# Exchanged matmul operands for the picked experts' weights, with a ScalarE copy of one one-hot table

## The chip, the core and the metric

The kernel runs on one core of a Trainium2 chip. The metric is the device time of one launch in microseconds (us), taken as the median of several runs. The engines are TensorE (PE in the profile, PEld for its weight loads), VectorE (DVE), ScalarE (ACT), GpSimd (POOL) and SyncE (SP, which issues the DMAs).

## The reference, cut to what matters

The program is a stack of three blocks on 256 tokens of width 1024. The change touches the expert layer of the first block only, `peer`. Each token takes, for each of 8 heads, 16 of 16,384 experts, where an expert is a pair of keys out of 128 and 128:

```python
def peer(h, w_pq, sub_keys, expert_u, expert_v):
    def one(xb):                                            # 128 tokens
        q = (xb @ w_pq).reshape(PEER_BLOCK, PEER_HEADS, 2, PEER_DKH)
        s = jnp.einsum('thpd,hpkd->thpk', q, sub_keys)
        sv, si = lax.top_k(s, PEER_TOPK)                    # 16 keys of each side
        cand = sv[:, :, 0, :, None] + sv[:, :, 1, None, :]
        cidx = si[:, :, 0, :, None] * N_KEYS + si[:, :, 1, None, :]
        best, pos = lax.top_k(cand..., PEER_TOPK)           # 16 experts of a head
        eidx = jnp.take_along_axis(cidx, pos, axis=-1)
        g = jax.nn.softmax(best, axis=-1)
        act = jax.nn.gelu(jnp.einsum('thkd,td->thk', expert_u[eidx], xb))
        return jnp.einsum('thk,thkd->td', g * act, expert_v[eidx])
```

## The kernel before, in words

The kernel does not gather experts. It multiplies all 128 x 128 experts with the tokens: `up(j)` makes the products of the 128 experts that have second key `j` (24 matmuls of 256 columns, since each product is made of three, high by high, high by low, low by high), ScalarE takes the gelu, and the result stands in `H[first key, j, token]`. Column `j` is then multiplied by a weight that is zero for all but the picked experts, and a last pass multiplies by `expert_v`.

The weights come from one-hot tables. A column of picks (8 heads by 16 picks) lies on the 128 partitions. For four tokens, `prepare` lets VectorE write two tables of float16 into `oo[pick, which key, key, token]`: a one where the pick's first key (`oo[:, 0]`) or second key (`oo[:, 1]`) equals the column (line 957). It multiplies `oo[:, 1]` with the pick's weight, which stands as a high and a low float16 part, into `ow` (line 959, two instructions). `group` then makes, for each of the four tokens, a 128 x 128 table of weights in PSUM by two matmuls, high and low part: `oo[:, 0]` of the token is the stationary operand, `ow` the moving one. In both tables the token is the innermost index, so the 128 keys of one token stand 4 elements, 8 bytes, apart, and a matmul's moving operand spreads over 1,024 bytes of each partition. The helper `shared` (lines 281 to 291) asks for one load of the stationary operand for both matmuls.

There are 64 groups (256 tokens by four). They lie between the 92 calls of `up` for `j` = 36 to 127; with `GR = 82` most calls have a `prepare` ahead and a `group` behind them (64 of 82), and the others have none. `PD = 1` puts a group one call behind its `prepare`. `drain` multiplies a finished PSUM table into `H`: VectorE for the columns that have their gelu already (lines 942 and 945), ScalarE copies the rest (line 948). A call of `up` needs its weights split: ScalarE rounds a loaded tile (line 302, tile `wh`), VectorE subtracts (line 306, tile `wl`). There are two buffers of each, so a split waits until TensorE is done with the call before last. Line 989 and 992 are the gelu, line 990 multiplies it with weights that are there already.

The code is recorded in program order, and a scheduler of the framework sets the final order of each engine's queue; each engine then works strictly in that order. `oo`, `ow` and the gelu's tile `k` share one pool of 6 buffers.

Of the kernel before, what the change touches and what calls it, by code (L numbers as in the profile page):

```python
# [12 lines left out]
F16 = mybir.dt.float16  # L13
U32 = mybir.dt.uint32
AF = mybir.ActivationFunctionType
OP = mybir.AluOpType
# [3 lines left out]
P = 128  # L20
# [239 lines left out]
class Kern:  # L260
# [16 lines left out]

    def mm(self, out, l, r, start=True, stop=True):
        self.nc.tensor.matmul(out, l, r, start=start, stop=stop, skip_group_check=True)  # L279

    def shared(self, l, jobs):

        t = self.nc.tensor
        for n, (out, r, start, stop) in enumerate(jobs):
            if n == 0:
                first = t.matmul(out, l, r, start=start, stop=stop, skip_group_check=True).ins  # L286
            else:
                t.add_instruction(mybir.InstMatmult(  # L288
                    name=self.nc.get_next_instruction_name(), engine=first.engine, start_tensor_calc=start,
                    stop_tensor_calc=stop, tile_size=first.tile_size, tile_position=first.tile_position,  # L290
                    bass_skip_group_check=True, ldweights=False, ins=[t.lower_ap(r), first.ins[1]],
                    outs=[t.lower_ap(out)]))

    def split(self, src, shape, hi="act", lo="dve"):
        d = self.SS(shape)
# [544 lines left out]
    def peer(self, ys, gb):  # L840


        nc, tc, I = self.nc, self.tc, self.I
        st = ExitStack()
        pool = st.enter_context(tc.tile_pool(name="pe", bufs=1, reuse_waits="tile"))
# [15 lines left out]
        W2 = pool.tile([P, 2, T], F16, name="W2")  # L861
# [76 lines left out]
        def drain():  # L938
            nonlocal toks
            pg, ts = pend.pop(0)  # L940
            pv = pg.rearrange("p (t j) -> p j t", t=4)
            nc.vector.scalar_tensor_tensor(H1[:, :, ts], pv[:, :NJ1], 1.0 / WS, H1[:, :, ts], op0=OP.mult, op1=OP.mult)
            m = cols - NJ1
            if m:
                nc.vector.scalar_tensor_tensor(H2[:, :m, ts], pv[:, NJ1:cols], 1.0 / WS, H2[:, :m, ts],
                                               op0=OP.mult, op1=OP.mult)
            if cols < NKEY:
                nc.scalar.activation(H2[:, m:, ts], pv[:, cols:], AF.Copy, scale=1.0 / WS)
            toks = ts.stop

        def prepare(t0):
            ts = slice(t0, t0 + 4)
            B = [P, P, 4]
            oo = pool.tile([P, 2, P, 4], F16, tag="k2", name="oo", bufs=6)
            ow = pool.tile([P, 2, P, 4], F16, tag="k2", name="ow", bufs=6)
            for i in (1, 0):
                nc.vector.tensor_tensor(oo[:, i], iota, IJ[:, i, None, ts].to_broadcast(B), op=OP.is_equal)
            for h in range(2):
                nc.vector.tensor_tensor(ow[:, h], oo[:, 1], W2[:, h, None, ts].to_broadcast(B), op=OP.mult)
            ready.append((oo, ow, ts))  # L960

        def group():
            oo, ow, ts = ready.pop(0)
            pg = self.bank()
            for i in range(4):
                self.shared(oo[:, 0, :, i], [(pg[:, i * P:(i + 1) * P], ow[:, h, :, i], h == 0, h == 1)
                                             for h in range(2)])
            pend.append((pg, ts))
            if len(pend) > LAG:
                drain()  # L970
# [10 lines left out]
        n, ready = 0, []  # L981
        for j in range(NJ1, NKEY):
            while n < 64 and n * GR < (j + 1 - NJ1 - GD) * 64:
                prepare(4 * n)
                n += 1
            pa = up(j, "dve" if j % PLO else "pool")
            if toks:
                ga = K1([P, T], F32)
                nc.scalar.activation(ga[:, :toks], pa[:, :toks], AF.Gelu)
                nc.vector.tensor_tensor(Hj(j)[:, :toks], ga[:, :toks], Hj(j)[:, :toks], op=OP.mult)  # L990
            if toks < T:
                nc.scalar.activation(Hj(j)[:, toks:], pa[:, toks:], AF.Gelu)
            cols = j + 1
            while len(ready) > (PD if n < 64 else 0):
                group()
            if n == 64 and not ready and pend:
                drain()
            if toks == T and j >= NKEY - VP:
                part(order[len(parted)])
# [1046 lines left out]
```

## Time and profile before

| | |
|---|---|
| median of 3 runs | 1917.75 us (1917.72 to 1919.15) |
| profiled execution | 1914.85 us, span 1913.1 us |
| TensorE busy | 1847.9 us (97%) |
| VectorE busy | 1304.5 us (68%) |
| ScalarE busy | 970.0 us (51%) |
| GpSimd busy | 176.9 us (9%) |

The profile is of one execution, and its own time is 1914.85 us. A record of a matmul lasts longer than the matmul holds the array: successive records overlap, so the distance from start to start is what a matmul costs in a full queue. In rows of matmuls the moving operand stands first behind the arrow and the stationary one second. Weight loads have records of their own (PEld), which also overlap.

### The profile page before, as it was taken

The numbers are of one execution on the slowest core, as the hardware profiler recorded it, in microseconds if no ns is written. First come the engines' busy times: TensorE is split into PE (matmuls) and PEld (weight loads), VectorE is DVE, ScalarE is ACT, GpSimd is POOL, SyncE is SP. The second block draws the span as 40 slices with busy tenths as digits, with TensorE's granted clock in tenths as the row PEclk, the third lists the DMA queues.
The fourth block names the chain that finished last, engine by engine and source line by source line (L and its number), as shares of the span: only waits on it lengthen the run. The fifth ranks groups of instructions, "written<-read, shape, count | busy, mean of one in ns | idle before, by whom it ended". The sixth has DMA issues, their size and how long they took to land.

```text
span 1913.1 us, 32724 instructions
## 1 busy us (share of the span) xinstructions
PE 1847.9 (97%) x12634; PEld 1645.1 (86%) x12634; DVE 1304.5 (68%) x3029; ACT 970.0 (51%) x1792; POOL 176.9 (9%) x119
## 2 busy tenths in 40 slices
PE   7999989999999999999999999998999999989998
PEld 6775579999999999888888789987999899879997
DVE  4536668987777887555555666677787656767785
ACT  4535444443444444544444546455666564456663
POOL 0000003320000000000000003320100033200000
PEclk9999999999999999999999999999999999999999
DMA  8732544543444445655555654313666234125671
GB/s 306 252 110 89 172 149 141 180 167 125 150 145 151 147 146 166 207 189 190 188 188 180 218 180 129 122 56 100 201 226 224 89 111 133 67 78 176 196 231 59
DMA packets 85100, 302.92 MB, mean 158 GB/s; under 512 B 10096, under 2 KB 10992, under 8 KB 84816
## 3 DMA queue, kind: packets, MB, share of 16 engines
q1 hardware_dynamic: 84944, 300.83, 48.0%
q8 instruction: 99, 1.62, 0.3%
q14 instruction: 57, 0.47, 0.1%
HBM read 298.56 MB, written 2.10 MB: 157 GB/s over the span
## 4 chain that ended last, share of the span: by engine, by line
PE 83%; DVE 11%; ACT 3%; DMA 1%; issue 1%; SPq 0%; POOLq 0%; POOL 0%; DVEq 0%; ACTq 0%
PE b L274 21%; PE b L276 21%; PE b L275 21%; PE b L279 13%; DVE wl L306 3%; PE b L286 2%; PE b L288 2%; PE b L1171 1%; PE b L537 1%; ACT wh L302 1%; PE b L1362 1%; DVE eq L1102 0%; DMA raw<-in_wv 0%; DVE tm L1035 0%; DVE u L1991 0%
## 5 line engine op out<-in xcount | busy, mean ns | idle before, releaser
L302 ACT ACTIVATE wh<-raw 128x1024 fp32r<-128x1024 f32 x457 | 483.8, 1060 | 562.1 <-PE b L275 265.9
L306 DVE TENSOR_TENSOR wl<-raw,wh 128x1024 fp32r<-128x1024 f32 x414 | 523.8, 1266 | 269.0 <-ACT wh L302 268.5
L276 PE MATMUL b<-r,wl 128*128 128x256 f32 (+1 forms) x1216 | 345.1, 284 | 9.8 <-DVE wl L306 9.8
L274 PE MATMUL b<-r,wh 128*128 128x256 f32 (+1 forms) x1216 | 351.0, 289 | 0.0
L275 PE MATMUL b<-r,wh 128*128 128x256 f32 x1152 | 323.1, 280 | 0.0
L274 PE MATMUL b<-hh,wh 128*128 128x256 f32 x1056 | 301.6, 286 | 1.8 <-DVE ast L1687 1.8
L276 PE MATMUL b<-hh,wl 128*128 128x256 f32 x1056 | 299.6, 284 | 1.8 <-DVE wl L306 1.7
L275 PE MATMUL b<-hl,wh 128*128 128x256 f32 x1056 | 298.6, 283 | 0.0
L276 PEld LDWEIGHTS b<-r,wl 128*128 128x128 f32 x1216 | 230.3, 189 | 12.6 <-DVE wl L306 11.0
L274 PEld LDWEIGHTS b<-r,wh 128*128 128x128 f32 x1216 | 231.4, 190 | 3.2 <-issue 1.5
L306 POOL TENSOR_TENSOR wl<-raw,wh 128x1024 fp32r<-128x1024 f32 x43 | 106.2, 2470 | 1240.0 <-ACT wh L302 960.1
L275 PEld LDWEIGHTS b<-r,wh 128*128 128x128 f32 x1152 | 218.4, 190 | 0.0
L274 PEld LDWEIGHTS b<-hh,wh 128*128 128x128 f32 x1056 | 202.2, 191 | 4.6 <-DVE ast L1687 2.3
L276 PEld LDWEIGHTS b<-hh,wl 128*128 128x128 f32 x1056 | 202.2, 191 | 3.1 <-DVE wl L306 3.0
L275 PEld LDWEIGHTS b<-hl,wh 128*128 128x128 f32 x1056 | 202.3, 192 | 1.4
L275 PE MATMUL b<-wl,k 128*128 128x512 f32 x492 | 194.8, 396 | 0.8 <-DVE wl L306 0.8
L274 PE MATMUL b<-wh,k 128*128 128x512 f32 x492 | 194.8, 396 | 0.0
L276 PE MATMUL b<-wh,k 128*128 128x512 f32 x492 | 194.6, 395 | 0.0
L275 PEld LDWEIGHTS b<-wl,k 128*128 128x128 f32 x492 | 92.4, 188 | 23.7 <-DVE wl L306 1.5
L274 PEld LDWEIGHTS b<-wh,k 128*128 128x128 f32 x492 | 92.4, 188 | 22.6 <-ACT wh L302 0.3
L276 PEld LDWEIGHTS b<-wh,k 128*128 128x128 f32 x492 | 92.4, 188 | 22.3
L1991 DVE SCALAR_TENSOR_TENSOR u<-b,vec,u 128x255 f32<-128x255 f32 (+1 forms) x176 | 84.3, 479 | 9.1 <-ACT u L1989 6.5
(493 smaller groups left out, 3091.8 us busy)
## 6 DMA issues: line engine op xcount, KB each, us to landing
raw<-in_eu SPq DMA_DIRECT2D x128, 512.0 KB, 3.9
raw<-in_ev SPq DMA_DIRECT2D x128, 512.0 KB, 3.5
raw<-in_fi SPq DMA_DIRECT2D x88, 512.0 KB, 4.4
raw<-in_w_ada SPq DMA_DIRECT2D x48, 512.0 KB, 5.6
raw<-in_wi SPq DMA_DIRECT2D x48, 512.0 KB, 3.8
raw<-in_fo SPq DMA_DIRECT2D x44, 512.0 KB, 4.6
raw<-in_w SPq DMA_DIRECT2D x16, 512.0 KB, 6.2
raw<-in_w_pq SPq DMA_DIRECT2D x16, 512.0 KB, 4.2
```

The lines of the kernel that those rows point to most:

```text
L274: mm(out, L.hi, R.hi, start=start, stop=False, skip_group_check=True)
L275: mm(out, L.hi, R.lo, start=False, stop=False, skip_group_check=True)
L276: self.lastmm = mm(out, L.lo, R.hi, start=False, stop=stop, skip_group_check=True)
L279: self.nc.tensor.matmul(out, l, r, start=start, stop=stop, skip_group_check=True)
L286: first = t.matmul(out, l, r, start=start, stop=stop, skip_group_check=True).ins
L288: t.add_instruction(mybir.InstMatmult(name=self.nc.get_next_instruction_name(), engine=first.engine, start_tensor_calc=start, stop_tensor_ ...
L302: nc.scalar.activation(dst.hi, src, AF.Copy)
L306: e.tensor_tensor(dst.lo, src, dst.hi.bitcast(F32), op=OP.subtract)
L537: nc.tensor.matmul(pa[32 * j:32 * j + 32, :P], self.s2[:, 4 * h + k], wa[:, k, m * P:(m + 1) * P], start=(k == 0), stop=(k == 3), tile_pos ...
L1171: nc.tensor.matmul(pa[32 * j:32 * j + 32], self.s2[:, k], wa[:, j % 2 * 512:(j % 2 + 1) * 512], start=(k == 0), stop=(k == KD - 1), tile_p ...
L1362: nc.tensor.transpose(pt[:, sc * P:(sc + 1) * P], Pm[:, sc * P:(sc + 1) * P], self.ident)
L1991: nc.vector.scalar_tensor_tensor(u[:, g, j:], src[:, :T - j], self.v2("fc", (2 - j) * 44 + i), u[:, g, j:], op0=OP.mult, op1=OP.add)
```

## The change

The operands change places. The weights are now multiplied into the first key's table (`oo[:, 0]`), and `ow` becomes the stationary operand, in its old layout with 4 elements between the keys of a token. The plain table of the second key moves; ScalarE first copies it into a new tile `oc[pick, token, key]`, in which the 128 keys of a token lie side by side (256 bytes). `oc` has a pool of 3 buffers of its own. `shared` goes, and the ordinary helper `mm` makes the eight matmuls of a group, each with its own stationary operand. The sums are the same.

```diff
-    def shared(self, l, jobs):
...
             for h in range(2):
-                nc.vector.tensor_tensor(ow[:, h], oo[:, 1], W2[:, h, None, ts].to_broadcast(B), op=OP.mult)
-            ready.append((oo, ow, ts))
+                nc.vector.tensor_tensor(ow[:, h], oo[:, 0], W2[:, h, None, ts].to_broadcast(B), op=OP.mult)
+            oc = pool.tile([P, 4, P], F16, tag="oc", name="oc", bufs=3)
+            nc.scalar.activation(oc, oo[:, 1].rearrange("p i t -> p t i"), AF.Copy)
+            ready.append((oc, ow, ts))
...
             for i in range(4):
-                self.shared(oo[:, 0, :, i], [(pg[:, i * P:(i + 1) * P], ow[:, h, :, i], h == 0, h == 1)
-                                             for h in range(2)])
+                for h in range(2):
+                    self.mm(pg[:, i * P:(i + 1) * P], ow[:, h, :, i], oo[:, i], start=h == 0, stop=h == 1)
```

In the new program lines stand 13 lower up to `prepare` and 10 or 11 lower behind it: 302 and 306 become 289 and 293, 942, 945 and 948 become 929, 932 and 935, 957 and 959 become 944 and 946, 989, 990 and 992 become 978, 979 and 981. The copy to `oc` is line 948 of the new program.

TensorE's queue at the first group, before (the end of a call of `up`, then weight loads and matmuls in pairs):

```order
L276 MATMUL b_4894<-r_2441,wl_4891 128x256
L286 LDWEIGHTS oo_4844
L286 MATMUL b_4920<-ow_4845,oo_4844 128x128
L288 LDWEIGHTS oo_4844
L288 MATMUL b_4920<-ow_4845,oo_4844 128x128
L286 LDWEIGHTS oo_4844
L286 MATMUL b_4920<-ow_4845,oo_4844 128x128
```

The same place of the new program:

```order
L276 MATMUL b_4898<-r_2441,wl_4895 128x256
L279 LDWEIGHTS ow_4845
L279 MATMUL b_4924<-oc_4850,ow_4845 128x128
L279 LDWEIGHTS ow_4845
L279 MATMUL b_4924<-oc_4850,ow_4845 128x128
L279 LDWEIGHTS ow_4845
L279 MATMUL b_4924<-oc_4850,ow_4845 128x128
```

The number of loads and of matmuls is the same, and both programs load weights ahead of each matmul, the one with `shared` too.

VectorE's queue over one group in the middle of the stretch, before (`H1` and `H2` are the two parts of `H`):

```order
L942 SCALAR_TENSOR_TENSOR H1_2627<-b_6416,H1_2627 128x36x4
L957 TENSOR_TENSOR oo_6428<-iota_2622,IJ_2618 128x512
L990 TENSOR_TENSOR H2_4843<-k1_6412,H2_4843 128x84
L945 SCALAR_TENSOR_TENSOR H2_4843<-b_6222,H2_4843 128x33x4
L957 TENSOR_TENSOR oo_6428<-iota_2622,IJ_2618 128x512
L959 TENSOR_TENSOR ow_6429<-oo_6428,W2_2619 128x512 x2
L306 TENSOR_TENSOR wl_6490<-raw_6487,wh_6489 128x1024
```

The same place of the new program:

```order
L929 SCALAR_TENSOR_TENSOR H1_2627<-b_6468,H1_2627 128x36x4
L944 TENSOR_TENSOR oo_6480<-iota_2622,IJ_2618 128x512
L979 TENSOR_TENSOR H2_4843<-k1_6464,H2_4843 128x84
L932 SCALAR_TENSOR_TENSOR H2_4843<-b_6268,H2_4843 128x33x4
L944 TENSOR_TENSOR oo_6480<-iota_2622,IJ_2618 128x512
L293 TENSOR_TENSOR wl_6546<-raw_6543,wh_6545 128x1024
L946 TENSOR_TENSOR ow_6481<-oo_6480,W2_2619 128x512 x2
```

The split of the weights (`wl`) now stands ahead of the two multiplications into `ow`.

ScalarE's queue at the same place, before:

```order
L302 ACTIVATE wh_6436<-raw_6434 128x1024
L989 ACTIVATE k1_6371<-b_6346 128x84
L992 ACTIVATE H2_4843<-b_6346 128x172
L302 ACTIVATE wh_6489<-raw_6487 128x1024
L989 ACTIVATE k1_6412<-b_6387 128x84
L992 ACTIVATE H2_4843<-b_6387 128x172
L948 ACTIVATE H2_4843<-b_6222 128x59x4
L302 ACTIVATE wh_6542<-raw_6540 128x1024
```

The same place of the new program:

```order
L289 ACTIVATE wh_6490<-raw_6488 128x1024
L978 ACTIVATE k1_6421<-b_6396 128x84
L981 ACTIVATE H2_4843<-b_6396 128x172
L948 ACTIVATE oc_6431<-oo_6425 128x512
L289 ACTIVATE wh_6545<-raw_6543 128x1024
L978 ACTIVATE k1_6464<-b_6439 128x84
L981 ACTIVATE H2_4843<-b_6439 128x172
L948 ACTIVATE oc_6486<-oo_6480 128x512
L935 ACTIVATE H2_4843<-b_6268 128x59x4
L289 ACTIVATE wh_6600<-raw_6598 128x1024
```

Each copy to `oc` stands behind the gelu of a call and ahead of the next copy out of PSUM and the next split.

## Rows read from the trace of the kernel before

**Rows 1.** The page: busy us, share of the span, instructions; TensorE's granted clock.
```profile
PE 1847.9 (97%) x12634; PEld 1645.1 (86%) x12634; DVE 1304.5 (68%) x3029; ACT 970.0 (51%) x1792; POOL 176.9 (9%) x119
PEclk9999999999999999999999999999999999999999
```
**Rows 2.** Busy time by stretch: the 92 calls, the groups, their end; then clock, DMA.
```profile
448.66:770.00 321.34, 321.34 (x2721) 317.24 (x2721) 246.71 (x564) 147.91 (x332) 0.00 (x0) 1.00 0.46 149
454.00:738.70 284.70, 284.70 (x2411) 280.60 (x2410) 221.58 (x520) 130.52 (x293) 0.00 (x0) 1.00 0.45 147
700.00:738.00 38.00, 38.00 (x324) 37.26 (x323) 32.76 (x71) 16.18 (x39) 0.00 (x0) 1.00 0.46 149
```
**Rows 3.** Timeline of TensorE around one group: start us, us, engine, line, what.
```profile
604.18 0.28 PE L275 MATMUL b<-r,wh 128*128 128x256 f32 x1
604.18 0.19 PEld L276 LDWEIGHTS b<-r,wl 128*128 128x128 f32 x1
604.30 0.28 PE L276 MATMUL b<-r,wl 128*128 128x256 f32 x1
604.41 0.29 PE L286 MATMUL b<-ow,oo 128*128 128x128 f16 x1
604.52 0.30 PE L288 MATMUL b<-ow,oo 128*128 128x128 f16 x1
604.52 0.12 PEld L286 LDWEIGHTS <-oo 128*128 128x128 f16 x1
604.64 0.30 PE L286 MATMUL b<-ow,oo 128*128 128x128 f16 x1
...
605.23 0.30 PE L288 MATMUL b<-ow,oo 128*128 128x128 f16 x1
605.28 0.37 PE L274 MATMUL b<-r,wh 128*128 128x256 f32 x1
605.49 0.28 PE L275 MATMUL b<-r,wh 128*128 128x256 f32 x1
```
**Rows 4.** Instructions on tile oo: duration ns min/median/max, first and last start.
```profile
L288 PEld LDWEIGHTS <-oo x256: 112/117/138, 454.2 to 738.6; 128*128 128x128 f16 x128
```
**Rows 5.** Timeline of TensorE in the last pass, matmuls of 512 columns.
```profile
999.97 0.40 PE L276 MATMUL b<-wh,k 128*128 128x512 f32 x1
1000.20 0.40 PE L274 MATMUL b<-wh,k 128*128 128x512 f32 x1
```
**Rows 6.** Timeline of TensorE, one moving column, new weights each; then those loads.
```profile
133.61 0.36 PE L279 MATMUL b<-half,qsq 128*128 128x1 f32 x2
133.83 0.36 PE L279 MATMUL b<-ones,qsq 128*128 128x1 f32 x2
...
L279 PEld LDWEIGHTS b<-ones,qsq x16: 190/192/192, 131.5 to 134.8; 128*128 128x128 f32 x16
```
**Rows 7.** Timeline of VectorE and ScalarE around the group; idle time before in brackets.
```profile
601.78 0.31 DVE L942 SCALAR_TENSOR_TENSOR H<-b,H 128x144 f32<-128x144 f32 x1 [0.60 <-PE b L288]
...
603.78 1.22 DVE L306 TENSOR_TENSOR wl<-raw,wh 128x1024 fp32r<-128x1024 f32 x1
605.57 0.31 DVE L942 SCALAR_TENSOR_TENSOR H<-b,H 128x144 f32<-128x144 f32 x1 [0.57 <-PE b L288]
...
602.89 0.34 ACT L948 ACTIVATE H<-b 128x196 f32<-128x196 f32 x1 [0.61 <-DVE H L945]
604.54 1.06 ACT L302 ACTIVATE wh<-raw 128x1024 fp32r<-128x1024 f32 x1 [1.32 <-PE b L275]
```
**Rows 8.** Waits from 454 to 740 us: total us, times, longest.
```profile
ACT wh L302 <- PE b L275: 76.7, 63, 2.5
...
DVE H L942 <- PE b L288: 31.2, 56, 2.2
```
**Rows 9.** Instructions by line and shape, ScalarE, 128x512: count, busy us, mean ns.
```profile
L302 ACT ACTIVATE wth<-raw 128x512 fp32r<-128x512 f32 x46 | 26.0, 618 | 0.6 <-DMA raw<-in_ev 0.6
L1303 ACT ACTIVATE Dm<-Dm,tiny 128x512 f32<-128x512 f32 x16 | 10.6, 713 | 4.4 <-DVE tiny L1299 4.3
```

More of the change, by code (lines that the diff above doesn't have):

```diff
@@ L279, in mm @@
         self.nc.tensor.matmul(out, l, r, start=start, stop=stop, skip_group_check=True)
-    def shared(self, l, jobs):
[L283 to L292, printed above, removed]
     def split(self, src, shape, hi="act", lo="dve"):
```

## Prediction

> **What bounds the kernel now.** I read the page first: TensorE is busy for 97% of the span, and its clock is granted in full throughout [rows 1]. An average over stages with different limits proves little, so the next view is busy time by stretch. In the 321 us of the 92 calls of `up`, TensorE is busy for every microsecond, with a granted clock of 1.00 (the 2.4 GHz level); VectorE is busy for 77% of it and ScalarE for 46%, DMA for 0.46 [rows 2]. So in this stage TensorE's queue is the time, and a change is worth what it takes out of that queue, as long as VectorE and ScalarE keep up.
>
> Next I read TensorE's queue around one group [rows 3]. The starts of the `up` matmuls, 256 columns of 4 bytes, are 0.12 us apart (604.18, 604.30). Within the group the eight starts run from 604.41 to 605.23: seven steps in 0.82 us, 117 ns each, for matmuls of only 128 columns. The last one costs more: from 605.23 to the second matmul of the next call (605.49) are 0.26 us for it and one matmul of 118 ns, so it takes some 140 ns. A group costs 7 x 117 + 140 = 0.96 us, and 64 of them 61 us. The stretch agrees: 321.3 us less 92 x 24 matmuls x 118 ns (260.5 us) leaves 60.8 us [rows 2, 3].
>
> Is it the load or the moving operand that takes 117 ns? **The load:** its record has a median of 117 ns [rows 4], which looks like the step. But in a queue where each matmul moves one column and has new weights, so that only loads count, pairs come every 0.22 us, one load per 112 ns, while each load's record lasts 192 [rows 6]. So some 80 ns of a load's record overlap its neighbours, and of the float16 record some 117 - 80 = 37 ns are left as its time on the array (an estimate from these rows). **The move:** 128 keys 8 bytes apart spread over 1,024 bytes of a partition, and 256 columns of 4 bytes are 1,024 bytes too. Both take 117 to 118 ns. That is what a limit by bytes passed over would give, and I take it as the cause. It is inferred: no row shows a float16 operand that moves without gaps.
>
> **The change part by part.** *The exchanged operands.* A line through 512 columns in 0.23 us [rows 5] and 256 in 118 ns gives 0.44 ns a column and some 4 ns over, so 128 columns without gaps take 61 ns. If the load (37 ns) stays hidden under the move, a step is 61 ns. The last matmul of a group keeps its 140 ns, because the 112 ns load of the next call's weights starts behind it and outlasts the move [rows 3, 6]. Saved: 64 x 7 x (117 - 61) ns = 25.1 us. The ends: if bytes alone limited a move, 256 bytes would be over before the load is, the step would be the load's 37 ns, and 35.8 us would go (to 1882 us); a step of 55 ns, between the two, gives 27.8 us. If the load isn't hidden, the step is 61 + 37 = 98 ns, and 8.5 us go. I take 61, since under the present step the load is hidden, and under the 118 ns of `up` a load of 112 ns is hidden as well [rows 3, 6].
>
> The Trainium skill speaks against this gain. "SBUF — State Buffer", section Specifications (TRN2), says that lines are 16 bytes and that two accesses to a line suffice for full bandwidth. Keys 8 bytes apart make two accesses, so by that rule the present move is not slowed at all, and the sum would be 0 instead of 25 us. The equal steps of rows 3 speak for the bytes; the rule keeps the chance of a rival below.
>
> *`shared` goes.* It costs nothing: the loads that it should have saved are in the trace, 256 on the line of the second matmul [rows 4]. The new program also has 512. The price of losing it would have been 256 loads.
>
> *The copies on ScalarE.* 64 of 128x512. The nearest rows are 618 and 713 ns [rows 9]; I take 0.63 us, 40 us in all, and twice that if the 8-byte gaps of the source cost there too. ScalarE has 130.5 us of work in the 284.7 us with groups [rows 2] and sits idle for 1.2 us on average ahead of a split, 76.7 us in 63 waits on TensorE [rows 8]. A copy fits there. It waits for VectorE's first table, and queued behind it on ScalarE are the copy out of PSUM and the split `wh`. In the cycle shown ScalarE is idle from 603.23 to 604.54 [rows 7], VectorE writes the first table right behind the instruction of 601.78, and the group that needs `oc` comes one call later, so I cost this at nothing. If that cover went, each copy would delay `wl` by up to 0.63 us.
>
> *VectorE* has the same instructions. Between two ends of groups it works from 601.78 to 605.00 and then idles 0.57 us until TensorE has finished the group [rows 7]; in all it waits 31.2 us there [rows 8]. The time that TensorE gives up, 0.39 us a group, comes out of this idle time. At the end of the stage VectorE's part is larger: from 700 to 738 it is busy 32.76 of 38.00 us [rows 2]. Nine groups lie there, so TensorE needs 3.5 us less and 1.7 us of slack are left; some calls will wait for `wl`. In the new order `wl` stands ahead of the two `ow`, while now it starts behind them at 603.78 and ends at 605.00, 0.28 us before the call that starts at 605.28 [rows 3, 7]. I allow 1 us for such waits; the low end has none, and the high end has 3 us.
>
> *The rest.* The loads of `raw` arrive at 0.46 of the DMA engines' time [rows 2] and need 8% more rate. Behind the stage TensorE is the bound again, so all that follows moves forward.
>
> *Sum.* 25.1 - 1 = 24.1 us. The profiled execution, 1914.85 us, becomes 1890.7 us. It lies 2.9 us below the median of the runs, so the median becomes 1917.75 - 24.1, about 1893.6 us.
>
> **The rivals.** *The load doesn't hide.* With a move of 61 ns, a load that cannot run beside it makes the step 98 ns: 8.5 us less, 1909 us. For it speaks that no row shows a load beside so short a move; against it, that 37 ns fit under 61. In the Trainium skill, "TensorE: Matmul & The Clock Gate", section Back-to-back issue gap, a stream of such pairs is given 81 ns; by that figure 16 us would go, 1902 us.
>
> *The move is not what takes 117 ns.* If it is the alternation of load and matmul (a load starts when the matmul before it starts, 604.52, and the next matmul starts when its record ends, 604.64 [rows 3]), the contiguous operand changes nothing and ScalarE's copies hide: 1918 us. Against it: the matmul of 604.30 starts while its load, from 604.18 for 0.19 us, is still on record [rows 3], so the end of a record holds nothing back. This is also what the rule of the lines would give.
>
> *Slower: the copies stand in the splits' way.* The step stays at 117 ns, and each copy waits so long for VectorE that it starts within 0.63 us of the moment when TensorE frees `wh`. Then the split starts late, `wl` behind it, and beyond the 0.28 us of slack TensorE waits: 64 x (0.63 - 0.28) = 22 us, 1940 us. It decides from a start of the copy that uses up the 1.2 us of idle time. Such a chain is there already (ScalarE waits 0.61 us for VectorE's line 945 at 602.89 [rows 7]), but ahead of idle time.
>
> **How the numbers follow.** The step of about 61 ns: 64%, from 1888 (near 55 ns, no waits, and 2 us of scatter between runs) to 1897 us. A shorter step, down to 37 ns: 3%, 1882 to 1888 us. The load beside it not hidden, wholly or in part: 15%, 1897 to 1909 us. No change: 13%, 1914 to 1921 us. Slower: 5%, up to 1940 us. The step near 61 ns and the load not hidden hold 79%, and a part of the shorter steps comes in, so the range is 1887 to 1909 us. A measurement of this kernel tells 0.2%, 3.8 us, from no change. Faster by more than that: 82%; within: 13%; slower: 5%.
>
> **What would show it.** In the profile after, starts within a group some 61 ns apart (98 or 117 for the rivals); 1.00 busy on TensorE in a stage 24 us shorter; 64 copies of about 0.63 us on ScalarE whose idle time before the split falls; VectorE's wait for the end of the group down from 31 us to about 10. The prediction is wrong if the steps stay at 117 ns, or if TensorE shows waits for `wl` or for `oc` of more than 3 us.

## The result and the profile after

The changed kernel takes 1891.03 us in the median of 4 runs (1887.24 to 1895.56), the kernel before beside it 1918.22 us. The ratio is 0.986, 95% interval 0.984 to 0.988: 27 us, 1.4%, faster. A second set of 5 runs gave 1890.11 us (0.986, 0.984 to 0.988). Forecast were 1893.6 us in a range of 1887 to 1909. The profiled execution after has 1893.5 us and a span of 1891.7 us; its lines below stand against those of an execution of 1914.85 us before, so the profiles differ by 21.4 us where the medians differ by 27: the profile before lies 3.4 us below its median, the one after 2.5 us above.

First the page: busy us, share of the span and instructions by engine, and TensorE's granted clock. They answer [rows 1].

```profile
PE 1823.5 (96%) x12634; PEld 1621.5 (86%) x12634; DVE 1305.4 (69%) x3029; ACT 1004.2 (53%) x1856; POOL 176.6 (9%) x119
PEclk9999989999999999999999999999999999999999
```

TensorE has the same 12634 matmuls and loads and is busy for 24.4 us less. ScalarE has 64 instructions and 34 us more. VectorE has the same instructions and the same busy time.

Busy time by stretch, to be read like [rows 2] (us of the stretch, then busy us and instructions on PE, PEld, DVE, ACT and POOL, granted clock, DMA share, GB/s): the 92 calls of `up`, the groups, and the last 34 us of the groups.

```profile
448.66:745.00 296.34, 296.04 (x2728) 292.92 (x2728) 247.39 (x563) 182.51 (x396) 0.00 (x0) 1.00 0.49 161
455.90:714.50 258.60, 258.30 (x2414) 255.18 (x2413) 223.03 (x522) 162.98 (x355) 0.00 (x0) 1.00 0.49 162
680.00:714.00 34.00, 33.70 (x316) 33.05 (x313) 31.52 (x73) 21.47 (x49) 0.00 (x0) 1.00 0.48 156
```

TensorE is still busy for all but 0.3 us, with its clock granted in full (the 2.4 GHz level), so its queue is still the time of the stage. VectorE fills 86% of the stretch with groups and 93% of the last 34 us, where it filled 78% and 86% before: it is now close to being the bound itself.

The timeline of TensorE, VectorE and ScalarE around one group (start, duration, engine, line, what; equal instructions behind one another are one row, from the first's start to the last's end). It answers [rows 3] and [rows 7].

```profile
592.06 0.28 PE L276 MATMUL b<-r,wl 128*128 128x256 f32 x1
592.10 0.75 DVE L946 TENSOR_TENSOR ow<-oo,W 128x512 f16<-128x512 f16 x2
592.18 0.48 PEld L279 LDWEIGHTS <-ow 128*128 128x128 f16 x8
592.18 0.64 PE L279 MATMUL b<-oc,ow 128*128 128x128 f16 x8
...
592.31 1.06 ACT L289 ACTIVATE wh<-raw 128x1024 fp32r<-128x1024 f32 x1 [1.19 <-issue]
592.60 0.19 PEld L274 LDWEIGHTS b<-r,wh 128*128 128x128 f32 x1
592.63 0.36 PE L274 MATMUL b<-r,wh 128*128 128x256 f32 x1
...
592.83 0.28 PE L275 MATMUL b<-r,wh 128*128 128x256 f32 x1
...
592.86 0.31 DVE L929 SCALAR_TENSOR_TENSOR H<-b,H 128x144 f32<-128x144 f32 x1
```

From the first start of the group to the start of the next call's first matmul are 0.45 us (592.18 to 592.63); in [rows 3] they are 0.87 (604.41 to 605.28). The single starts in the trace are 84 ns apart at the first step, then 55, 56, 56, 56, 56, 56, and 28 from the last one to the call's first matmul, which needs 0.20 instead of 0.12 us up to the next. Within a group the step has fallen from 117 to 56 ns. VectorE reaches the end of the group (592.86) with no idle time at all.

The instructions on tile `oc`: duration in ns (min/median/max), first and last start, what the copy waited for, and who waited for tile or copy.

```profile
L948 ACT ACTIVATE oc<-oo x64: 659/672/691, 451.1 to 710.8; 128x512 f16<-128x512 f16 x64
...
  DVE oo L944: 1.3, 4
...
  ACT wh L289: 16.9, 18
```

And the waits from 448.66 to 745 us, which answer [rows 8] (who, for whom: total us, times, longest).

```profile
ACT wh L289 <- PE b L275: 33.8, 40, 1.5
ACT wh L289 <- issue: 33.5, 29, 1.5
...
DVE wl L293 <- ACT wh L289: 17.4, 27, 2.0
ACT wh L289 <- ACT oc L948: 13.9, 16, 0.9
...
DVE H L929 <- PE b L279: 4.0, 7, 1.5
...
PE b L279 <- DVE ow L946: 0.3, 1, 0.3
```

The last row is all that TensorE's matmuls wait for in the stage. These rows cover all 92 calls, and [rows 8] only the stretch with groups. Over all calls before, `wh` waits for TensorE 88.3 us in 72 cases. ScalarE's whole idle time ahead of `wh` falls from 115.4 to 84.9 us, of which 13.9 are now waits for a copy.

### The profile page after: what moved, and what is told of

Its sections match the earlier page's. It is cut to its first block, busy times and chain, and to the rows that moved or that the text cites. A ratio compares the mean times of both kernels' runs of the same rounds, so it can differ in the third digit from the quotient of the medians.

```text
span 1891.7 us, 32791 instructions
## 1 busy us (share of the span) xinstructions
PE 1823.5 (96%) x12634; PEld 1621.5 (86%) x12634; DVE 1305.4 (69%) x3029; ACT 1004.2 (53%) x1856; POOL 176.6 (9%) x119
## 4 chain that ended last, share of the span: by engine, by line
PE 82%; DVE 12%; ACT 3%; DMA 1%; issue 1%; SPq 0%; POOLq 0%; POOL 0%; DVEq 0%; ACTq 0%
PE b L274 22%; PE b L276 21%; PE b L275 21%; PE b L279 14%; DVE wl L293 3%; PE b L1160 1%; DMA raw<-in_wv 1%; ACT wh L289 1%; PE b L524 1%; PE b L1351 1%; DMA raw<-in_w_ada 1%; DVE eq L1091 0%; DVE tm L1024 0%; DVE u L1980 0%; DVE jt L741 0%
## 5 line engine op out<-in xcount | busy, mean ns | idle before, releaser
L275 PEld LDWEIGHTS b<-wl,k 128*128 128x128 f32 x492 | 92.4, 188 | 24.7 <-DVE wl L293 2.6
```

The lines of the kernel that those rows point to most:

```text
L275: mm(out, L.hi, R.lo, start=False, stop=False, skip_group_check=True)
```

## The experiments

**The exchange without the copy.** Does it matter which of the two one-hots moves, or only how its numbers lie? Against the changed kernel:

```
-            oc = pool.tile([P, 4, P], F16, tag="oc", name="oc", bufs=3)
-            nc.scalar.activation(oc, oo[:, 1].rearrange("p i t -> p t i"), AF.Copy)
-            ready.append((oc, ow, ts))
+            ready.append((oo, ow, ts))
...
-                    self.mm(..., ow[:, h, :, i], oo[:, i], ...)
+                    self.mm(..., ow[:, h, :, i], oo[:, 1, :, i], ...)
```

> The change without its copy: operands exchanged (ow stationary), but the second key's table moves as it lies, 8 bytes between keys; no ScalarE copy. Theory 'spacing of the moving operand': starts inside a group stay 117 to 118 ns apart and the time is that of the kernel before, 1918 us within 3. Rival 'the exchange itself' (which table is stationary, one load per matmul asked for plainly): the steps fall to 57 ns as in the changed kernel, and the time is about 1890 us.

It took 1917.97 us (10 runs), ratio 1.000, interval 0.999 to 1.001. TensorE's timeline around a group:

```profile
591.89 1.12 PE L279 MATMUL b<-oo,ow 128*128 128x128 f16 x8
592.76 0.37 PE L274 MATMUL b<-r,wh 128*128 128x256 f32 x1
```

Group and gap are those of before, 0.87 us, with single steps of 117 to 120 ns behind a first one of 110. With the plain one-hot moving, and the weighted ones loaded as weights, nothing is gained as long as the moving keys lie 8 bytes apart. So the gain needs the copy's layout, and the exchange alone gives none of it. Whether a copy would do without the exchange was not run; the two weighted tables, twice as many numbers, would then have to be copied.

**The copy without the exchange.** 64 copies that nobody reads, in the kernel before. It tests the rival in which the copies stand in the splits' way:

```
+            oc = pool.tile([P, 4, P], F16, tag="oc", name="oc", bufs=3)
+            nc.scalar.activation(oc, oo[:, 1].rearrange("p i t -> p t i"), AF.Copy)
             ready.append((oo, ow, ts))
```

> The kernel before with the 64 copies to oc added on ScalarE, which nobody reads. Theory 'the copies hide': 1918 us, not more than 3 us above the kernel before, TensorE still 1.00 busy through the stage, and the wait of the split for TensorE shorter by some 40 us. Rival 'the copies stand in the splits' way': above 1925 us, with TensorE waiting for wl. The new tile also moves what lies behind it in memory: if that is what holds back ScalarE's first square after the last pass (line 724 of the changed kernel, 12.1 us of waiting for TensorE), the same wait shows here and costs 2 to 3 us.

It took 1918.33 us (10 runs), ratio 1.000, interval 0.999 to 1.001. Busy time of the 92 calls:

```profile
448.66:770.00 321.34, 321.34 (x2709) 317.25 (x2708) 243.95 (x563) 183.21 (x392) 0.00 (x0) 0.99 0.45 147
```

and the waits at the copy, from 454 to 770 us:

```profile
ACT wh L302 <- ACT oc L961: 13.1, 15, 0.9
ACT oc L961 <- DVE oo L957: 10.4, 35, 0.7
```

ScalarE has 35 us more work than in [rows 2], and splits do wait for copies (13.1 us, with 10.4 us of copies waiting for VectorE ahead of that). The splits' wait for TensorE falls from 76.7 to 30.2 us (454 to 740 us), about as expected. TensorE stays busy for every microsecond, and the price of the copies alone is nothing that ten runs can tell.

**The spacing between the keys.** The copy is written with 4, then 6 bytes from key to key, in one buffer, and a group is issued in the call that prepares it. Groups now wait for their tables (with 4 bytes TensorE waits 12.2 us for `ow`, and its loads 18.5 us), so only the step inside a group is compared. The times, 1913.78 and 1928.06 us in one run each, hold these waits and say nothing of the step.

```
-PD = 1
+PD = 0
...
-            oc = pool.tile([P, 4, P], F16, tag="oc", name="oc", bufs=3)
-            nc.scalar.activation(oc, oo[:, 1].rearrange("p i t -> p t i"), AF.Copy)
+            oc = pool.tile([P, 4, P, 2], F16, tag="oc", name="oc", bufs=1)
+            nc.scalar.activation(oc[:, :, :, 0], oo[:, 1].rearrange("p i t -> p t i"), AF.Copy)
```

(and `oo[:, i, :, 0]` as the moving operand; with `3` in place of `2` for 6 bytes).

> The changed kernel, with the copy written to [token, key] at a spacing of 4 bytes from key to key instead of 2, in one buffer, each group issued one call later than it is prepared no longer but in the same call (so the groups may wait for their copy; only the step of the one-hot matmuls inside a group is compared). Theory 'bytes passed over': 118 ns for 128 columns at 8 bytes is 0.115 ns per byte, so 512 bytes take 59 ns: steps of 57 to 60 ns, next to the changed kernel's 56 to 57. Rival 'any gap doubles it': 118 ns again. Rival 'two numbers in 16 bytes are enough': 56 ns.

> The same with a spacing of 6 bytes. Theory 'bytes passed over': 768 bytes at 0.115 ns give 88 ns per step. Rival 'any gap doubles it': 118 ns. Rival 'two numbers in 16 bytes are enough': 56 ns. A rival by whole words of 4 bytes would give the same as at 8 bytes, 118 ns, or the same as at 4.

One group with 4 bytes (719.61) and the call behind it:

```profile
719.61 0.67 PE L279 MATMUL b<-oc,ow 128*128 128x128 f16 x8
720.08 0.36 PE L274 MATMUL b<-r,wh 128*128 128x256 f32 x1
```

and one with 6 bytes:

```profile
730.31 0.90 PE L279 MATMUL b<-oc,ow 128*128 128x128 f16 x8
730.99 0.36 PE L274 MATMUL b<-r,wh 128*128 128x256 f32 x1
```

The single steps inside groups, from the starts in the traces, without the first step of a group:

```
bytes from key to key     2    4    6    8
bytes passed over       256  512  768  1024
median step, ns          56   59   90   118
0.115 ns per byte        29   59   88   118
```

From 4 to 8 bytes the step is proportional to the bytes passed over; at 2 bytes something else holds it at 56 ns. The rival that any gap doubles the step, and the one that two numbers in 16 bytes are enough, both fall: by them the steps at 4 and 6 bytes would be equal.

**Halves.** What holds the step at 56 ns, the move of 128 columns or the load beside it? Every one-hot matmul is cut in two of 64 columns with a load each. Its sums differ from the kernel's; it is read for its times alone.

```
-                    self.mm(pg[:, i * P:(i + 1) * P], ow[:, h, :, i], oo[:, i], ...)
+                    for c in range(0, P, 64):
+                        self.mm(pg[:, i * P + c:i * P + c + 64], ow[:, h, :, i], oo[:, i, c:c + 64], ...)
```

> The changed kernel with every one-hot matmul cut into two of 64 columns, each with its own load of the same weights: 16 per group, the same columns in all. If the move of the columns sets the step of 56 ns, 64 columns take 28 to 29 ns, a group lasts as long as now and the time stays at 1888 to 1896 us. If the load of the 128x128 weights (or the issue of a load and matmul) sets it, the step stays at 50 to 57 ns, a group gets 8 x 50 to 57 ns longer, and the kernel 64 times that: 26 to 29 us more, some 1916 to 1920 us.

```profile
590.01 0.72 PE L279 MATMUL b<-oc,ow 128*128 128x64 f16 x16
590.57 0.36 PE L274 MATMUL b<-r,wh 128*128 128x256 f32 x1
```

The steps are 33 to 34 ns, a group 0.56 us instead of 0.45, the time 1898.88 us in one run. Neither expectation was met exactly, but the question is answered: a 128x128 float16 load fits into 33 ns, so it does not hold a step of 56 ns, and the move of the columns does. At 64 columns 5 ns more than half a step are left, the load's or a fixed cost of a matmul; that stays open.

**A wait given back behind the last pass.** The aligned traces show more than the stage. Taking the same matmul in both, the profile after is 1.1 us behind the one before at 447 us, 24.7 us ahead at 743 us, and only 20.9 us ahead at 1134 us (times of the profile before). Of these 3.8 us, 2.9 are lost in the last 22 us, and the other 0.9 earlier in the last pass. (The 1.1 us ahead of the stage, where the queues are the same, differ from execution to execution.) ScalarE's timeline after (in brackets the idle time before, and what ended it):

```profile
1107.19 0.63 ACT L724 ACTIVATE jj<-r 128x512 bf16<-128x512 f32 x1 [12.12 <-PE b L276]
...
1110.23 0.40 ACT L759 ACTIVATE jdg<-ident,rq 128x128 f32<-128x128 f32 x1 [1.70 <-DVE rq L410]
```

and TensorE's behind it:

```profile
1110.68 2.05 PE L279 MATMUL b<-jdg,r 128*128 128x128 f32 x16 [2.88 <-ACT jdg L759]
```

The first square of the next block (line 724) waits until TensorE has finished the last pass, though it reads `r` alone; TensorE then idles for the tile `jdg`, a diagonal that ScalarE makes from the square's sum. Before, ScalarE waited here for VectorE only, and TensorE not at all for `jdg`:

```profile
ACT jj L737 <- DVE r L762: 6.1, 2, 3.5
```

My first theory was that `oc` takes memory in which the next block's first tiles lie. So `oc` was put into the pool of `H2`:

```
-            oc = pool.tile([P, 4, P], F16, tag="oc", name="oc", bufs=3)
+            oc = g2s.tile([P, 4, P], F16, tag="oc", name="oc", bufs=3)
```

> The changed kernel with oc taken from the pool that holds H2 instead of the pool of oo, so that the tiles of the first two pools lie where they lay in the kernel before. Theory 'place in memory': ScalarE's first square after the last pass no longer waits 12 us for TensorE, TensorE no longer idles 2.9 us for the scaled identity (line 759), and the time is 2 to 3 us below the changed kernel, about 1888 us. Rival 'chance or shifted loads': the wait stays, and the time is that of the changed kernel, about 1891 us.

The wait stayed, with 11.9 us, and the theory fell: 1888.4 us (6 runs, 1886.77 to 1900.12), ratio 0.987, interval 0.984 to 0.989. It is in the exchange without a copy as well (9.4 us, though TensorE waits only 0.8 us for `jdg` there) and not in the copies without an exchange (6.0 us, for `r`). So it comes with the exchange. The unchanged kernel in the same set:

> The changed kernel as it is, on the same chip as the one above, for comparison: 1887 to 1896 us as in its four runs so far; by the theory on the place in memory TensorE idles 2.9 us for line 759 in this profile again, by the rival it may not.

It showed the wait again, 11.5 us (1890.11 us, 5 runs). The addresses in the built programs point to a cause. The six buffers that `oo` and `ow` share with the later splits of `H` are handed out as they come free. With the operands exchanged they come free in another order, so the last five parts of `H`, which TensorE reads until the very end of the pass, lie in other buffers. `jss`, the 8-byte sum that the first square writes, has the same address in all programs, and lies within one of the six:

```
program                           jss at   last tile there     ScalarE's wait for TensorE
before, copies without exchange   77216    6th-last part       none
exchange without copy             77216    5th-last part       9.4 us
after, oc elsewhere               77216    2nd-last part       12.1, 11.9 us
```

The next run lets the block ask for one small tile first, so that `jss` gets another address (62880), where no part of `H` lies:

```
         self.classes = {128: 40, 512: 8, 1024: 34, 4096: 3}
+        self.S([P, 16])
```

> The changed kernel with one small tile asked for first in the pool of the second block, so that the sums of the first squares (the 8-byte tile jss) lie elsewhere in memory. In the changed program they lie inside the buffer of a split of H1 that TensorE reads until the last pass ends; in the program before, that buffer was one that TensorE was done with. Theory: the 12.1 us wait of ScalarE's first square for TensorE goes, TensorE's idle time for the following diagonal (2.9 us) goes, and the time falls by 2 to 3 us, to 1885 to 1889 us. Rival: the wait has another cause and stays, 1888 to 1892 us.

ScalarE's timeline there:

```profile
1098.19 0.63 ACT L724 ACTIVATE jj<-r 128x512 bf16<-128x512 f32 x1 [3.17 <-DVE r L749]
...
1104.10 0.40 ACT L759 ACTIVATE jdg<-ident,rq 128x128 f32<-128x128 f32 x1 [1.63 <-DVE rq L410]
```

The wait for TensorE is gone: the diagonal starts at 1104.10 instead of 1110.23, TensorE does not wait for it any more, and from 1089 to 1138 us the profile gains 2.1 us on the changed kernel's, of the 2.9 lost. The other tile that the square writes, `jj`, keeps its address in this program, so it is the place of `jss` that makes the wait. What this is worth is not shown in the whole time, and the 1885 to 1889 us expected were not met: 1890.31 us (5 runs, 1883.67 to 1895.19), ratio 0.984, interval 0.982 to 0.987, which can't be told from the changed kernel.

## Why the prediction was right

**The bound.** TensorE's queue was the time of the stage, and what left the queue left the time. The stage gained 25.8 us between the profiles (1.1 behind to 24.7 ahead), for 24.1 forecast. From the first group on, where the profile after is 1.8 us behind, it gained 26.5.

**The cause of the 117 ns.** It was inferred from two equal steps, at 1,024 bytes each. The points at 4 and 6 bytes show it as a line through bytes. The Trainium skill's rule that stood against it ("SBUF — State Buffer", section Specifications (TRN2): for full bandwidth a 16-byte line needs two accesses or more), read as in the prediction, does not hold for a moving operand here: at 8 bytes there are two accesses to such a line, and 128 columns take 118 ns instead of 56. The same row of that table also has a penalty for each move to a new line, which the prediction left out. Between 4 and 8 bytes the lines touched (32, 48 and 64) grow as the bytes do, so a price by lines instead of bytes is a rival that these runs can't tell from it.

**The new step, 61 ns forecast.** Measured are 56. The forecast drew its line through moves of 4 bytes a column, and by the experiment on spacing such moves go by their bytes (59 ns for 128 columns). By bytes alone the 256 bytes of the copy would take 29 ns; what holds them at 56 is the columns, as the run of halves shows (33 ns for 64). No row of before shows that 128 columns cost nearly the same at 2 and at 4 bytes a column, so it is partly luck that the line came so near. The load hides, as assumed: where 37 ns were worked out for it, 33 are enough. The rival of 81 ns (the Trainium skill, "TensorE: Matmul & The Clock Gate", Back-to-back issue gap) is not borne out by any of these groups, with a load to each matmul at 56 ns apart, and 33 ns with half the columns.

**The ends of a group.** The last matmul was to keep 140 ns. It costs 28 + 202 - 118 = 112 ns. This is as long as the load of [rows 6], so the call's first load probably still outlasts the move, but less; no run changes that load alone. A cost not in the sum stands at the other end: the first step is 84 ns, not 56. Together a group is 84 + 6 x 56 + 112 = 532 ns, where the forecast had 7 x 61 + 140 = 567, and before it was 0.95 us by the stretch. 64 x 0.42 is 26.8 us; the forecast's 25.1 lies below it because its step is too long (36 ns a group) and its last matmul saves nothing (23 ns), while its first step saves 32 ns too much (it was 108 ns before, by single starts).

**The copies.** Forecast 0.63 us each and free. They take 0.672, more than forecast but not twice, and are free, shown by the run that has them alone. Their cover was in the main the idle time ahead of `wh`, 30.5 us less over the 92 calls, where the copies are busy for 42.9 us. Another part is ScalarE's wait for VectorE ahead of the copy out of PSUM, which falls from 58.0 to 26.3 us.

**VectorE.** Its wait for the end of a group was to fall from 31 us to about 10; it fell to 4.0. Waits of TensorE at the end of the stage were put at 1 us; there are 0.3. VectorE did keep up, with 93% of the last 34 us in use.

**What was missing.** That all behind the stage moves forward unchanged was wrong by 3.8 us, of which 2.9 are explained above. The edit changes when `oo` comes free, and that decides which buffer holds the last parts of `H`, and so when a square behind the pass may start. No view of the profile of before shows it, since that wait is not there; the addresses in the built program would have. So the errors of the sum cancel in part: 26.8 us saved instead of 25.1, 0.3 us of waits instead of 1, and 3.8 us given back instead of none, which makes 22.7 for 24.1. The medians differ by more, 27 us; why the executions behind them gained more than the profiled ones is not shown.

## What to carry to other kernels

Here the price of a moving float16 operand went by the bytes that it passes over, from 4 bytes between its numbers on (59, 90 and 118 ns for 128 columns), and by its columns without gaps (56 ns). Where TensorE is the bound and a small operand moves with gaps, a copy without gaps on an engine with idle time can be worth the difference; a spacing of 4 bytes already had nearly all of it in the step, and the order of the operands alone was worth nothing (1917.97 us). Before counting such a gain, check that the new step isn't held up by columns or loads, and how busy the other engines get: here VectorE is at 93% at the end of the stage, and a next cut of TensorE may show less. A change in who reads a shared buffer last moves tiles to other addresses, and can put a wait far behind the edited stage; the waits of the whole program are to be compared, not those of the stage.

## What the runs showed that I had not expected

One kernel's steps are not always the same. In the profile with `oc` in the pool of `H2`, the 256-column matmuls of `up`, 117 to 118 ns apart in nearly all of the profiles before and after, are 113 ns apart from 457 to 665 us, with the clock granted in full in both, and 118 again from there on. The same four starts, first there and then in the changed kernel:

```profile
560.68 0.28 PE L276 MATMUL b<-r,wl 128*128 128x256 f32 x1
560.79 0.28 PE L274 MATMUL b<-r,wh 128*128 128x256 f32 x1
560.91 0.28 PE L275 MATMUL b<-r,wh 128*128 128x256 f32 x1
561.02 0.28 PE L276 MATMUL b<-r,wl 128*128 128x256 f32 x1
```

```profile
560.74 0.28 PE L276 MATMUL b<-r,wl 128*128 128x256 f32 x1
560.86 0.28 PE L274 MATMUL b<-r,wh 128*128 128x256 f32 x1
560.98 0.28 PE L275 MATMUL b<-r,wh 128*128 128x256 f32 x1
561.10 0.28 PE L276 MATMUL b<-r,wl 128*128 128x256 f32 x1
```

Three steps take 0.34 us in the one and 0.36 in the other; over 1,500 matmuls that makes 6.3 us between the two profiles. The execution with `jss` moved has the shorter steps too, from 714 us to the end of the stage, and the one with 4 bytes between the keys has them in several short stretches. The 6.3 us are about the size of the scatter between runs of one kernel (1887 to 1896 us for the changed one). Whether it is its cause is not shown: both profiles of the changed kernel are of its longer executions (1893.5 and 1894.7 us), with some 118 ns nearly throughout, and what decides between 113 and 118 ns stays open.
